# Instance normalisation: deeper lag between loads and stores, two-pass variance, and work taken off GpSimd

## The chip, the cores and the metric

The kernel runs on one core of one Trainium2 chip. The metric is the device time of one execution in microseconds (us). The profile's span is about 1.8 us shorter than that time, because it leaves out what lies around the program.

## The reference, cut to what matters

```python
x = randn(8, 64, 32, 64, 64), float32          # 512 instances of 131072 elements
mean = x.mean over the last three axes
var = x.var over the last three axes
out = (x - mean) / sqrt(var + 1e-5)            # float32
```

The input is 268.4 MB and so is the output. Every element has to come in once and go out once: 536.9 MB.

## The kernel before

Both kernels cut the data in the same way. An instance is spread over 16 partitions, 8192 elements on each, so that a tile of 128 partitions by 8192 elements holds 8 instances and 4 MB. There are 64 tiles. Each is loaded, normalised in place and stored. Loads and stores are all issued on one queue, SyncE's. (The profile has short names for the engines: SP is SyncE, DVE VectorE, ACT ScalarE, POOL GpSimd, PE TensorE and PEld its weight loads; a q behind a name is the part of an engine that waits and issues.)

```python
    LAG = 2
    # ... cut ...
    data_pool = ctx.enter_context(tc.tile_pool(name="data", bufs=4))
    # ... cut ...
    c1 = F // 8
    c2 = F // 4
    norm_splits = [
        (nc.vector, 0, c1),
        (nc.scalar, c1, c2),
        (nc.gpsimd, c2, F),
    ]

    def issue_load(g):
        x_tiles = data_pool.tile([P, KPG, F], fp32, name="x_tiles")
        src = x_packed[g * KPG : (g + 1) * KPG].rearrange("k p f -> p k f")
        nc.sync.dma_start(out=x_tiles, in_=src)
        return x_tiles
    # ... cut ...
        for k in range(KPG):
            nc.vector.reduce_sum(
                out=psums[:, k, 0:1],
                in_=x_tiles[:, k, :],
                axis=mybir.AxisListType.X,
            )
    # ... cut ...
            nc.scalar.activation(
                out=sq_scratch,
                in_=x_tiles[:, k, :],
                func=mybir.ActivationFunctionType.Square,
                accum_out=psums[:, k, 1:2],
            )

```

The sum of every partition comes from VectorE and the sum of squares from ScalarE. A matmul with a block pattern adds up the 16 partitions of an instance and spreads the result over them. Six small operations make `scale` and `bias` (cut here). Then three engines share the normalisation, GpSimd with three quarters of the columns:

```python
        for k in range(KPG):
            for eng, lo, hi in norm_splits:
                if eng is nc.scalar:
                    nc.scalar.activation(
    # ... cut ...
                    )
                else:
                    eng.tensor_scalar(
                        out=x_tiles[:, k, lo:hi],
    # ... cut ...
                    )

    def issue_store(g, x_tiles):
        dst = out_packed[g * KPG : (g + 1) * KPG].rearrange("k p f -> p k f")
        nc.sync.dma_start(out=dst, in_=x_tiles)

    pending = {}
    for g in range(n_groups):
        x_tiles = issue_load(g)
        issue_compute(g, x_tiles)
        pending[g] = x_tiles
        if g >= LAG:
            issue_store(g - LAG, pending.pop(g - LAG))
    for g in range(n_groups - LAG, n_groups):
        issue_store(g, pending.pop(g))
```

The store of tile g-2 stands in the queue behind the load of tile g, and four tiles fit in the buffers.

## Time and profile before

| | before |
|---|---|
| time, median of 3 runs | 1251.63 us (1251.09 to 1252.23) |
| span of the profiled run | 1249.7 us |
| VectorE, ScalarE, GpSimd busy | 53%, 44%, 30% |
| the queue's transfers, share of 16 DMA engines' span | 99.7% |
| one tile in the steady state | 19.37 us = 8.39 MB at 433 GB/s |

These lines are from the page of the kernel before. They give the span; each engine's busy time; the DMA queue with its packets, megabytes and share of 16 DMA engines' time; and the three costliest groups of instructions: busy time, mean of one in ns, idle time just before them and what ended it.

```profile
span 1249.7 us, 1827 instructions
...
PE 35.7 (3%) x128; PEld 32.1 (3%) x128; DVE 659.2 (53%) x449; ACT 550.6 (44%) x258; POOL 380.3 (30%) x70
...
q1 hardware_dynamic: 18432, 536.88, 99.7%
...
L92 DVE TENSOR_REDUCE psums<-x_tiles 128x1 f32<-128x8192 f32 x64 | 555.9, 8686 | 492.9 <-DMA x_tiles<-in_x_dram 492.9
L100 ACT ACTIVATE sq_scratch<-x_tiles 128x8192 bf16<-128x8192 f32 x64 | 449.9, 7029 | 461.3 <-DMA x_tiles<-in_x_dram 461.3
L169 POOL TENSOR_SCALAR x_tiles<-x_tiles,scale,bias 128x6144 f32<-128x6144 f32 x64 | 379.4, 5929 | 855.4 <-DVE bias L149 634.4
```

No compute engine is full and the DMA engines are. The two engines that open a tile wait for loads (492.9 and 461.3 us in all).

The waits of the queue's own issuing engine in the kernel before (instruction, what it waited for, us in all, times, longest):

```profile
SPq L85 <- DMA out_dram<-x_tiles: 700.8, 60, 12.6
SPq L180 <- POOL x_tiles L169: 303.9, 64, 4.8
```

Loads (L85) wait until an earlier store has left its buffer. Stores (L180) wait for the engines that normalise, mostly GpSimd.

The end of the kernel before, in order of time: the last tile's part on GpSimd, and the last three stores, the last of them issued at the end of the interval, 1198.00 + 39.04 = 1237.04 us. It has to wait for GpSimd.

```profile
1198.00 39.04 SPq L180 DMA_DIRECT2D out_dram<-x_tiles  x3
...
1230.76 5.93 POOL L169 TENSOR_SCALAR x_tiles<-x_tiles,scale,bias 128x6144 f32<-128x6144 f32 x1 [13.42 <-ACT std L141]
```

And this is the table of windows of the kernel before. Its last two columns: the busy share of the 16 DMA engines, as a mean over the engines, and GB/s. (A packet counts in the window where it starts, so short windows scatter, and can show more than 1.)

```profile
core 0: us, PE busy (x) PEld busy (x) DVE busy (x) ACT busy (x) POOL busy (x), PEclk, DMA share, GB/s
0.00:60.00 60.00, 1.67 (x6) 1.50 (x6) 37.50 (x23) 34.66 (x15) 18.92 (x9) 1.00 0.98 410
60.00:500.00 440.00, 12.83 (x46) 11.53 (x46) 230.31 (x161) 190.41 (x92) 135.40 (x23) 1.00 1.00 432
...
1233.00:1237.00 4.00, 0.00 (x0) 0.00 (x0) 0.00 (x0) 0.00 (x0) 3.69 (x1) 1.00 0.31 131
1237.00:1241.00 4.00, 0.00 (x0) 0.00 (x0) 0.00 (x0) 0.00 (x0) 0.00 (x0) 1.00 0.92 393
1241.00:1245.00 4.00, 0.00 (x0) 0.00 (x0) 0.00 (x0) 0.00 (x0) 0.00 (x0) 1.00 1.22 524
1245.00:1249.00 4.00, 0.00 (x0) 0.00 (x0) 0.00 (x0) 0.00 (x0) 0.00 (x0) 1.00 0.36 156
```

From 1233 to 1237 us, while GpSimd finishes the last tile, the mean share is 0.31.

### The profile page before, as it was taken

To read this page: it belongs to the slowest core of one execution; us is meant where nothing else is said; L and a number is where in the kernel's file an instruction comes from. 1 tells how busy PE (TensorE), PEld (TensorE's weight loads), DVE (VectorE), ACT (ScalarE), POOL (GpSimd) and SP (SyncE) were. 2 spreads that over 40 slices of the span, in tenths; PEclk is the share of its full clock that TensorE was granted. 3 is DMA by queue.
4 is the path that set the end of the run, shared out by engine and by line. 5 is a ranking of instruction groups with operands and counts; after the bars stand their busy time and mean duration, and the time that the engine had idled before them with its cause. 6 is when DMAs were issued, how large, how long until landed. Compare 5 with 4: busy or idle time off the path is not lost.

```text
span 1249.7 us, 1827 instructions
## 1 busy us (share of the span) xinstructions
PE 35.7 (3%) x128; PEld 32.1 (3%) x128; DVE 659.2 (53%) x449; ACT 550.6 (44%) x258; POOL 380.3 (30%) x70
## 2 busy tenths in 40 slices
PE   0000000000000000000000000000000000000000
PEld 0000000000000000000000000000000000000000
DVE  5736455464554645546546455464554645646543
ACT  5535445354453544535435344354453544534432
POOL 2332332313323233232331322313323233132231
DMA  9999999999999999999999999999999999999998
GB/s 403 417 434 434 427 433 430 432 435 430 429 432 434 432 435 429 434 433 434 434 431 433 431 434 434 435 430 432 434 433 436 429 433 434 433 434 435 429 433 357
DMA packets 18444, 536.99 MB, mean 430 GB/s; under 512 B 2048, under 2 KB 2048, under 8 KB 2048
## 3 DMA queue, kind: packets, MB, share of 16 engines
q1 hardware_dynamic: 18432, 536.88, 99.7%
q14 instruction: 11, 0.09, 0.0%
q8 instruction: 1, 0.02, 0.0%
HBM read 268.44 MB, written 268.44 MB: 430 GB/s over the span
## 4 chain that ended last, share of the span: by engine, by line
DMA 74%; issue 16%; POOL 7%; DVE 1%; POOLq 1%; PE 0%; ACT 0%
DMA out_dram<-x_tiles 39%; DMA x_tiles<-in_x_dram 35%; POOL x_tiles L169 7%; DVE psums L92 1%; POOLq L221 0%; DVE x_tiles L169 0%; POOLq L169 0%; PE tot L108 0%; ACT std L141 0%; DVE scale L147 0%; DVE msq L128 0%; DVE me L117 0%; DVE bias L149 0%; DVE var_eps L131 0%
## 5 line engine op out<-in xcount | busy, mean ns | idle before, releaser
L92 DVE TENSOR_REDUCE psums<-x_tiles 128x1 f32<-128x8192 f32 x64 | 555.9, 8686 | 492.9 <-DMA x_tiles<-in_x_dram 492.9
L100 ACT ACTIVATE sq_scratch<-x_tiles 128x8192 bf16<-128x8192 f32 x64 | 449.9, 7029 | 461.3 <-DMA x_tiles<-in_x_dram 461.3
L169 POOL TENSOR_SCALAR x_tiles<-x_tiles,scale,bias 128x6144 f32<-128x6144 f32 x64 | 379.4, 5929 | 855.4 <-DVE bias L149 634.4
L161 ACT ACTIVATE x_tiles<-x_tiles,bias,scale 128x1024 f32<-128x1024 f32 x64 | 79.4, 1241 | 40.5 <-DVE bias L149 40.5
L141 ACT ACTIVATE std<-var_eps 128x1 f32<-128x1 f32 x64 | 13.0, 203 | 178.7 <-DVE var_eps L131 178.7
L108 PE MATMUL tot<-psums,ones_t 128*128 128x2 f32 x128 | 35.7, 348 | 1193.5 <-DVE psums L92 1193.5
L108 PEld LDWEIGHTS tot<-psums,ones_t 128*128 128x128 f32 x128 | 32.1, 311 | 1197.1 <-issue 1197.1
L169 DVE TENSOR_SCALAR x_tiles<-x_tiles,scale,bias 128x1024 f32<-128x1024 f32 x64 | 52.1, 813 | 2.5
L117 DVE TENSOR_SCALAR me<-tot 128x2 f32<-128x2 f32 x64 | 10.2, 160 | 47.5 <-PE tot L108 47.5
L147 DVE RECIPROCAL scale<-std 128x1 f32<-128x1 f32 x64 | 10.5, 164 | 21.8 <-ACT std L141 21.8
L100 ACT ACTIVATION_READ_ACCUMULATOR sq_scratch<-x_tiles 128x1 f32 x64 | 11.9, 187 | 0.0
L128 DVE TENSOR_TENSOR msq<-me 128x1 f32<-128x1 f32 x64 | 10.2, 159 | 2.2
L131 DVE SCALAR_TENSOR_TENSOR var_eps<-me,msq 128x1 f32<-128x1 f32 x64 | 10.2, 159 | 2.2
L149 DVE SCALAR_TENSOR_TENSOR bias<-me,scale 128x1 f32<-128x1 f32 x64 | 10.2, 159 | 2.2
L100 ACT ACT_TABLE_LOAD x1 | 1.3, 1283 | 0.8 <-PEq L207 0.8
L141 ACT ACT_TABLE_LOAD x1 | 1.3, 1283 | 0.0
L51 DVE MEMSET ones_t<- 128x128 f32 x1 | 0.2, 165 | 0.9 <-PEq L207 0.9
L53 POOL TENSOR_SCALAR_AFFINE_SELECT ones_t<-ones_t 128x128 f32<-128x128 f32 x1 | 0.3, 343 | 0.6 <-DVE ones_t L51 0.6
L62 POOL TENSOR_SCALAR_AFFINE_SELECT ones_t<-ones_t 128x128 f32<-128x128 f32 x1 | 0.3, 338 | 0.1
L207 POOL MEMSET const-float32-0.0<- 128x1 f32 x1 | 0.1, 98 | 0.3 <-issue 0.3
L207 POOL MEMSET const-bfloat16-1.0<- 128x1 bf16 x1 | 0.1, 101 | 0.0
L207 POOL MEMSET const-uint8-127<- 128x1 uint8 x1 | 0.1, 101 | 0.0
(1 smaller groups left out, 0.1 us busy)
## 6 DMA issues: line engine op xcount, KB each, us to landing
x_tiles<-in_x_dram SPq DMA_DIRECT2D x64, 4096.0 KB, 29.0
out_dram<-x_tiles SPq DMA_DIRECT2D x64, 4096.0 KB, 31.5
```

The source lines that it names most:

```text
L92: nc.vector.reduce_sum(out=psums[:, k, 0:1], in_=x_tiles[:, k, :], axis=mybir.AxisListType.X,)
L100: nc.scalar.activation(out=sq_scratch, in_=x_tiles[:, k, :], func=mybir.ActivationFunctionType.Square, accum_out=psums[:, k, 1:2],)
L108: nc.tensor.matmul(out=tot, lhsT=ones_t, rhs=psums, start=True, stop=True,)
L117: nc.vector.tensor_scalar(out=me2, in0=tot, scalar1=inv_F, scalar2=None, op0=mybir.AluOpType.mult,)
L128: nc.vector.tensor_mul(out=msq, in0=mean, in1=mean)
L131: nc.vector.scalar_tensor_tensor(out=var_eps, in0=e2, scalar=eps_f, in1=msq, op0=mybir.AluOpType.add, op1=mybir.AluOpType.subtract,)
L141: nc.scalar.activation(out=std, in_=var_eps, func=mybir.ActivationFunctionType.Sqrt,)
L147: nc.vector.reciprocal(out=scale, in_=std)
L149: nc.vector.scalar_tensor_tensor(out=bias, in0=mean, scalar=-1.0, in1=scale, op0=mybir.AluOpType.mult, op1=mybir.AluOpType.mult,)
L161: nc.scalar.activation(out=x_tiles[:, k, lo:hi], in_=x_tiles[:, k, lo:hi], func=mybir.ActivationFunctionType.Identity, scale=scale[:, k : ...
L169: eng.tensor_scalar(out=x_tiles[:, k, lo:hi], in0=x_tiles[:, k, lo:hi], scalar1=scale[:, k : k + 1], scalar2=bias[:, k : k + 1], op0=mybir ...
L207: nc = _bacc.Bacc("TRN2", target_bir_lowering=False, num_devices=1)
```

## The change

The intent is a shorter chain from a loaded tile to a ready one, GpSimd out of the stream, a variance computed from differences (meant to be more exact than E[x²] - mean²; not compared here), and more room between a load and its store: six buffers, and the store of tile g-4 behind the load of tile g. The instructions stand on every engine in program order.

```diff
-    LAG = 2                      (four data buffers)
+    SLOTS = 6                    (six data buffers)
...
-    nc.vector.reduce_sum(psums[:, k, 0:1], x_tiles)            # all columns
-    nc.scalar.activation(sq_scratch, x_tiles, Square, accum_out=psums[:, k, 1:2])
-    matmul, then me2, msq, var_eps, std (Sqrt), scale, bias
+        nc.vector.reduce_sum(out=sums[:, 0:1], in_=t[:, :cut])         # cut = F // 2
+        nc.scalar.activation(out=unused[:, cut:], in_=t[:, cut:],
+                             func=Act.Identity, accum_out=sums[:, 1:2])
+        nc.tensor.matmul(out=mean_ps, lhsT=avg, rhs=sums, start=True, stop=True)
+        nc.vector.tensor_reduce(out=neg_mean, in_=mean_ps, op=Alu.add, negate=True)
+        nc.scalar.activation(out=unused, in_=t, func=Act.Square,
+                             bias=neg_mean, accum_out=squares)
+        nc.tensor.matmul(out=var_ps, lhsT=avg, rhs=squares, start=True, stop=True)
+        nc.scalar.activation(out=std, in_=var_ps, func=Act.Sqrt, bias=eps_t)
+        nc.vector.reciprocal(out=scale, in_=std)
+        nc.vector.tensor_mul(out=bias, in0=neg_mean, in1=scale)
-    normalise: VectorE 1/8, ScalarE 1/8, GpSimd 3/4 of the columns
+        nc.vector.tensor_scalar(t[:, cut:], scale, bias)               # half
+        nc.scalar.activation(t[:, :cut], Identity, scale, bias)        # half
...
+    LAG = 4
+    with tc.manual_schedule():
+        for g in range(n_tiles + LAG):
+            if g < n_tiles:
+                tiles[g] = load(g)
+                compute(tiles[g])
+            if g >= LAG:
+                nc.sync.dma_start(out=out_t[g - LAG], in_=tiles.pop(g - LAG))
```

(Arguments are shortened, and cuts are marked with "..." .)

More of the change, by code (lines that the diff above doesn't have):

```diff
@@ L4 @@
 import concourse.tile as tile
-from concourse import bass_utils, mybir
+from concourse import mybir
 from concourse._compat import with_exitstack
@@ L18 @@
     fp32 = mybir.dt.float32
+    Alu = mybir.AluOpType
+    Act = mybir.ActivationFunctionType
     P = 128
@@ L29 @@
     F = n_elem // SPLIT
-    G = 8
-    KPG = G // IPT
-    n_groups = n_inst // G
-    LAG = 2
-    x_packed = x.rearrange("b c d h w -> (b c) (d h w)").rearrange(
+    n_tiles = n_inst // IPT
+    SLOTS = 6
+    x_t = x.rearrange("b c d h w -> (b c) (d h w)").rearrange(
         "(k i) (s f) -> k (i s) f", i=IPT, s=SPLIT
     )
-    out_packed = out.rearrange("b c d h w -> (b c) (d h w)").rearrange(
+    out_t = out.rearrange("b c d h w -> (b c) (d h w)").rearrange(
         "(k i) (s f) -> k (i s) f", i=IPT, s=SPLIT
@@ L44 @@
     singles = ctx.enter_context(tc.tile_pool(name="singles", bufs=1))
-    data_pool = ctx.enter_context(tc.tile_pool(name="data", bufs=4))
-    scratch_pool = ctx.enter_context(tc.tile_pool(name="scratch", bufs=2))
+    data_pool = ctx.enter_context(tc.tile_pool(name="data", bufs=SLOTS))
     stat_pool = ctx.enter_context(tc.tile_pool(name="stats", bufs=4))
-    psum_pool = ctx.enter_context(tc.tile_pool(name="psum", bufs=4, space=bass.MemoryType.PSUM))
-    ones_t = singles.tile([P, P], fp32)
-    nc.vector.memset(ones_t, 1.0 / SPLIT)
-    blk_pattern = [[-SPLIT, P // SPLIT], [0, SPLIT]]
+    psum_pool = ctx.enter_context(
+        tc.tile_pool(name="psum", bufs=2, space=bass.MemoryType.PSUM)
+    )
+    avg = singles.tile([P, P], fp32, name="avg")
+    nc.vector.memset(avg, 1.0 / n_elem)
     nc.gpsimd.affine_select(
-        out=ones_t,
-        in_=ones_t,
-        pattern=blk_pattern,
-        compare_op=mybir.AluOpType.is_ge,
+        out=avg,
+        in_=avg,
+        pattern=[[-SPLIT, IPT], [0, SPLIT]],
+        compare_op=Alu.is_ge,
         fill=0.0,
@@ L62 @@
     nc.gpsimd.affine_select(
-        out=ones_t,
-        in_=ones_t,
-        pattern=[[SPLIT, P // SPLIT], [0, SPLIT]],
-        compare_op=mybir.AluOpType.is_ge,
+        out=avg,
+        in_=avg,
+        pattern=[[SPLIT, IPT], [0, SPLIT]],
+        compare_op=Alu.is_ge,
         fill=0.0,
@@ L70 @@
     )
-    inv_F = 1.0 / F
-    c1 = F // 8
-    c2 = F // 4
-    norm_splits = [
-        (nc.vector, 0, c1),
-        (nc.scalar, c1, c2),
-        (nc.gpsimd, c2, F),
-    ]
-    def issue_load(g):
-        x_tiles = data_pool.tile([P, KPG, F], fp32, name="x_tiles")
-        src = x_packed[g * KPG : (g + 1) * KPG].rearrange("k p f -> p k f")
-        nc.sync.dma_start(out=x_tiles, in_=src)
-        return x_tiles
-    def issue_compute(g, x_tiles):
-        psums = stat_pool.tile([P, KPG, 2], fp32, name="psums")
-        for k in range(KPG):
-            nc.vector.reduce_sum(
-                out=psums[:, k, 0:1],
-                in_=x_tiles[:, k, :],
-                axis=mybir.AxisListType.X,
-            )
-            sq_scratch = scratch_pool.tile(
-                [P, F], mybir.dt.bfloat16, name="sq_scratch"
-            )
-            nc.scalar.activation(
-                out=sq_scratch,
-                in_=x_tiles[:, k, :],
-                func=mybir.ActivationFunctionType.Square,
-                accum_out=psums[:, k, 1:2],
-            )
-        tot = psum_pool.tile([P, KPG, 2], fp32, name="tot")
-        nc.tensor.matmul(
-            out=tot,
-            lhsT=ones_t,
-            rhs=psums,
-            start=True,
-            stop=True,
-        )
-        me2 = stat_pool.tile([P, KPG, 2], fp32, name="me2")
-        nc.vector.tensor_scalar(
-            out=me2,
-            in0=tot,
-            scalar1=inv_F,
-            scalar2=None,
-            op0=mybir.AluOpType.mult,
-        )
-        mean = me2[:, :, 0]
-        e2 = me2[:, :, 1]
-        msq = stat_pool.tile([P, KPG], fp32, name="msq")
-        nc.vector.tensor_mul(out=msq, in0=mean, in1=mean)
-        var_eps = stat_pool.tile([P, KPG], fp32, name="var_eps")
-        nc.vector.scalar_tensor_tensor(
-            out=var_eps,
-            in0=e2,
-            scalar=eps_f,
-            in1=msq,
-            op0=mybir.AluOpType.add,
-            op1=mybir.AluOpType.subtract,
-        )
-        std = stat_pool.tile([P, KPG], fp32, name="std")
-        nc.scalar.activation(
-            out=std,
-            in_=var_eps,
-            func=mybir.ActivationFunctionType.Sqrt,
-        )
-        scale = stat_pool.tile([P, KPG], fp32, name="scale")
-        nc.vector.reciprocal(out=scale, in_=std)
-        bias = stat_pool.tile([P, KPG], fp32, name="bias")
-        nc.vector.scalar_tensor_tensor(
-            out=bias,
-            in0=mean,
-            scalar=-1.0,
-            in1=scale,
-            op0=mybir.AluOpType.mult,
-            op1=mybir.AluOpType.mult,
-        )
-        for k in range(KPG):
-            for eng, lo, hi in norm_splits:
-                if eng is nc.scalar:
-                    nc.scalar.activation(
-                        out=x_tiles[:, k, lo:hi],
-                        in_=x_tiles[:, k, lo:hi],
-                        func=mybir.ActivationFunctionType.Identity,
-                        scale=scale[:, k : k + 1],
-                        bias=bias[:, k : k + 1],
-                    )
-                else:
-                    eng.tensor_scalar(
-                        out=x_tiles[:, k, lo:hi],
-                        in0=x_tiles[:, k, lo:hi],
-                        scalar1=scale[:, k : k + 1],
-                        scalar2=bias[:, k : k + 1],
-                        op0=mybir.AluOpType.mult,
-                        op1=mybir.AluOpType.add,
-                    )
@@ L178, in issue_store @@
-    def issue_store(g, x_tiles):
-        dst = out_packed[g * KPG : (g + 1) * KPG].rearrange("k p f -> p k f")
-        nc.sync.dma_start(out=dst, in_=x_tiles)
-    pending = {}
-    for g in range(n_groups):
-        x_tiles = issue_load(g)
-        issue_compute(g, x_tiles)
-        pending[g] = x_tiles
-        if g >= LAG:
-            issue_store(g - LAG, pending.pop(g - LAG))
-    for g in range(n_groups - LAG, n_groups):
-        issue_store(g, pending.pop(g))
+    eps_t = singles.tile([P, 1], fp32, name="eps_t")
@@ new lines, with load, compute @@
+    nc.vector.memset(eps_t, eps_f)
+    unused = singles.tile([P, F], mybir.dt.uint8, name="unused")
+    def load(g):
+        t = data_pool.tile([P, F], fp32, name="xt")
+        nc.sync.dma_start(out=t, in_=x_t[g])
+        return t
+    def compute(t):
+        cut = F // 2
+        sums = stat_pool.tile([P, 2], fp32, name="sums")
+        nc.vector.reduce_sum(
+            out=sums[:, 0:1], in_=t[:, :cut], axis=mybir.AxisListType.X
+        )
+        nc.scalar.activation(
+            out=unused[:, cut:],
+            in_=t[:, cut:],
+            func=Act.Identity,
+            accum_out=sums[:, 1:2],
+        )
+        mean_ps = psum_pool.tile([P, 2], fp32, name="mean_ps")
+        nc.tensor.matmul(out=mean_ps, lhsT=avg, rhs=sums, start=True, stop=True)
+        neg_mean = stat_pool.tile([P, 1], fp32, name="neg_mean")
+        nc.vector.tensor_reduce(
+            out=neg_mean,
+            in_=mean_ps,
+            axis=mybir.AxisListType.X,
+            op=Alu.add,
+            negate=True,
+        )
+        squares = stat_pool.tile([P, 1], fp32, name="squares")
+        nc.scalar.activation(
+            out=unused, in_=t, func=Act.Square, bias=neg_mean, accum_out=squares
+        )
+        var_ps = psum_pool.tile([P, 1], fp32, name="var_ps")
+        nc.tensor.matmul(out=var_ps, lhsT=avg, rhs=squares, start=True, stop=True)
+        std = stat_pool.tile([P, 1], fp32, name="std")
+        nc.scalar.activation(out=std, in_=var_ps, func=Act.Sqrt, bias=eps_t)
+        scale = stat_pool.tile([P, 1], fp32, name="scale")
+        nc.vector.reciprocal(out=scale, in_=std)
+        bias = stat_pool.tile([P, 1], fp32, name="bias")
+        nc.vector.tensor_mul(out=bias, in0=neg_mean, in1=scale)
+        nc.vector.tensor_scalar(
+            out=t[:, cut:],
+            in0=t[:, cut:],
+            scalar1=scale,
+            scalar2=bias,
+            op0=Alu.mult,
+            op1=Alu.add,
+        )
+        nc.scalar.activation(
+            out=t[:, :cut], in_=t[:, :cut], func=Act.Identity, scale=scale, bias=bias
+        )
@@ L194 @@
+    LAG = 4
+    tiles = {}
+    with tc.manual_schedule():
[5 more added lines that the diff above has]
+                nc.sync.dma_start(out=out_t[g - LAG], in_=tiles.pop(g - LAG))
 _INS = ['x', 'eps']
```

## The prediction

> **What bounds the kernel now.** The 16 DMA engines. The page's slice table shows DMA at nine tenths in all slices but the last; the queue table gives the one SP queue 99.7% of 16 engines' span, 536.9 MB at a mean 430 GB/s. No compute engine is near full (VectorE 53%, ScalarE 44%, GpSimd 30%); VectorE's big reductions idle 493 us waiting for loads (groups table). In the timeline a tile takes 19.37 us (reductions at 600.16 and 1219.84, 32 tiles apart): 8.39 MB per tile, 433 GB/s. The Trainium skill, "DMA: Bandwidth & Descriptors", section "Where 436 GB/s comes from", gives a fabric ceiling of 435.2 GB/s; this trace agrees. At that ceiling the bytes alone take 1233.6 us, so no schedule of the same bytes gains 2%.
>
> **Where the rest goes (windows table).** Start: 2 us before full rate; from 2 to 60 us a mean near 417 GB/s, some 2 us lost, part of it where three loads are done and the first store is only just issued (30 us). End: from 1233 to 1237 the DMA share is 0.31, because the last store waits for tile 63's chain (reduction 8.69, matmul and small operations 1.9, GpSimd 5.93 us): about 3 us lost. After the last packets near 1247.3 come 2.4 us of completion.
>
> **What the change does.** Bytes, packets, queue: unchanged. GpSimd's normalisation and the single-pass square go; sums and normalisation are split in halves over VectorE and ScalarE; the square needs the mean. Tiles follow one another in program order; only the next tile's sums start as each engine gets free. Estimates from before's durations:
> - sums: VectorE 4096 of 8192 elements, 4.4 us; ScalarE 3.8 us (1241 ns for 1024 and 7029 ns for 8192: about 0.83 ns each)
> - matmul, negated mean: 0.95 us
> - ScalarE square with accumulator read: 7.3 us
> - matmul, square root, reciprocal, bias: 1.45 us
> - normalisation: ScalarE half 3.8 us (VectorE half 2.3 to 3.2)
>
> The loop closes through ScalarE: 3.8 + 0.95 + 7.3 + 1.45 + 3.8 = 17.3 us per tile, 15.2 of them ScalarE (78% of the span). That is 2 us under the DMA's 19.37, so the chain stays hidden. The order on each engine shows two activation-table loads in all, so none in the chain.
>
> **On the critical path.** Only start and end. Five loads run unbroken (49 us) while tile 0 is ready near 31 us, so the dip goes. In steady state both kernels keep two or more 4 MB transfers queued: same rate. At the end stores 59 to 62 (39 us of DMA) stand between the last load and the last store and cover tile 63's 17 us: the hole goes. Gain 3.5 to 5 us, 0.3 to 0.4%.
>
> **Predicted: 1247.5 us, 8 in 10 between 1241 and 1252.** Faster by over 2%: 0.01; within 2%: 0.96; slower: 0.03.
>
> **What would show it.** DMA share about 99.8%; no hole before the last store; 19.3 to 19.4 us per tile; ScalarE 75 to 80% busy, VectorE near 40%, GpSimd near zero; ScalarE's sums waiting 1.5 to 2.5 us per tile for the load once the initial backlog is worked off; SP waiting on stores landing, hardly on compute.
>
> **What would make it wrong.** A compute chain over 19.4 us (slower VectorE half, long semaphore hops) would make it compute-bound with DMA share below 95%: 20 us per tile would be about 1290. Another DMA rate, from the all-load start, the all-store end or the other spacing of loads and stores, would move it by some 0.3% either way.

## The result

| | before | after |
|---|---|---|
| median of the runs made together (4 each) | 1251.66 us | 1251.43 us (1251.12 to 1251.57) |
| ratio after/before | | 0.9997, 95% interval 0.9983 to 1.0011 |
| span of the profiled run | 1249.7 us | 1249.9 us |
| VectorE, ScalarE, GpSimd busy | 53%, 44%, 30% | 37%, 77%, 0% |
| last store issued | 1237.04 us | 1218.83 us |

A ratio here was made, with its interval, from the fast runs of both kernels in the same rounds, so it is not quite the ratio of the medians. The time lies inside the predicted range (1241 to 1252), and "the same within 2%" was right. But the gain of 3.5 to 5 us that the prediction counted on is not there: it is 0.2 us, with an interval from 2.1 us faster to 1.4 us slower. That the time still lies in the range is no support for this gain: the range reached up to the time of the kernel before.

The same lines of the page, for the kernel after:

```profile
span 1249.9 us, 1770 instructions
...
PE 73.7 (6%) x256; PEld 64.1 (5%) x256; DVE 467.1 (37%) x322; ACT 960.3 (77%) x386; POOL 0.9 (0%) x6
...
q1 hardware_dynamic: 18432, 536.88, 99.7%
...
L103 ACT ACTIVATE unused<-xt,neg_mean 128x8192 uint8<-128x8192 f32 x64 | 455.8, 7122 | 99.5 <-DVE neg_mean L95 99.5
L83 DVE TENSOR_REDUCE sums<-xt 128x1 f32<-128x4096 f32 x64 | 282.8, 4419 | 156.3 <-DMA xt<-in_x_dram 156.3
L86 ACT ACTIVATE unused<-xt 128x4096 uint8<-128x4096 f32 x64 | 231.3, 3614 | 84.8 <-DMA xt<-in_x_dram 84.8
```

The compute side came out as foreseen. ScalarE is the busiest engine and still waits for loads (84.8 us at its first instruction of a tile). The first instruction of the second and third tile on ScalarE in the kernel after (start, duration), and then of two tiles of the steady state (in brackets the idle time before and what ended it):

```profile
31.40 3.60 ACT L86 ACTIVATE unused<-xt 128x4096 uint8<-128x4096 f32 x1
...
48.37 3.60 ACT L86 ACTIVATE unused<-xt 128x4096 uint8<-128x4096 f32 x1
```

```profile
600.43 3.62 ACT L86 ACTIVATE unused<-xt 128x4096 uint8<-128x4096 f32 x1 [1.56 <-DMA xt<-in_x_dram]
...
619.75 3.62 ACT L86 ACTIVATE unused<-xt 128x4096 uint8<-128x4096 f32 x1 [1.48 <-DMA xt<-in_x_dram]
```

From 31.40 to 48.37 us is 16.97 us, the chain of one tile without waiting for a load. In the steady state a tile comes every 19.3 to 19.4 us, and ScalarE idles 1.5 us for it.

The queue's own waits and its last issues in the kernel after. Long waits of stores for compute are left at six stores (83.2 us in all; before, 303.9 us at all 64 for GpSimd alone), and the last five stores are all issued by 1172.09 + 46.74 = 1218.83 us, 18 us earlier than before:

```profile
SPq L77 <- DMA out_dram<-xt: 1069.7, 58, 19.5
SPq L135 <- DVE xt L114: 83.2, 6, 26.9
```

```profile
1172.09 46.74 SPq L135 DMA_DIRECT2D out_dram<-xt  x5
```

And the same table of windows, for the kernel after:

```profile
0.00:60.00 60.00, 2.91 (x10) 2.51 (x10) 19.20 (x14) 43.03 (x17) 0.89 (x6) 1.00 0.97 411
60.00:500.00 440.00, 28.41 (x98) 24.55 (x98) 176.53 (x123) 360.54 (x148) 0.00 (x0) 1.00 1.00 432
...
1233.00:1237.00 4.00, 0.00 (x0) 0.00 (x0) 0.00 (x0) 0.00 (x0) 0.00 (x0) 1.00 1.02 442
1237.00:1241.00 4.00, 0.00 (x0) 0.00 (x0) 0.00 (x0) 0.00 (x0) 0.00 (x0) 1.00 0.95 410
1241.00:1245.00 4.00, 0.00 (x0) 0.00 (x0) 0.00 (x0) 0.00 (x0) 0.00 (x0) 1.00 0.59 254
1245.00:1249.00 4.00, 0.00 (x0) 0.00 (x0) 0.00 (x0) 0.00 (x0) 0.00 (x0) 1.00 0.19 82
```

The hole between 1233 and 1237 us is gone (1.02 instead of 0.31), exactly as predicted. In its place the share falls off at the end: 0.59 and 0.19 between 1241 and 1249 us, with nothing left to issue and nothing to wait for. The start is no better either: 411 GB/s over the first 60 us against 410. So the question is where the 3 us of the hole went.

### What a mean over 16 engines hides

A transfer of this kernel is carried by all 16 DMA engines, eight packets of 32 KB on each. The Trainium skill, "DMA: Bandwidth & Descriptors", section "Why a DMA increments its semaphore by 16 and not by 1", says that every engine that takes part adds its own increment to the transfer's semaphore (the counter that a waiting engine watches) when its share has landed. The trace agrees: it holds 2048 such landings for 128 transfers, 16 for each. They do not say which engine each came from, but the first and the last of the 16 can be read for every transfer. This table is worked out from those records (in us of the span; the zero of each run is set by the first transfer's last landing, which released the first instruction, or, where nothing is computed, by the 0.84 us that lie between the last landing and the end of the span):

```
                        transfer before the last      last transfer
                        first engine, last engine     first engine, last engine
before                  1233.35       1239.17         1247.65       1248.83
after                   1233.09       1239.37         1242.77       1249.03
```

In the kernel before the fastest engine was done with the store of tile 62 at 1233.35 us and then waited for the last store, issued at 1237.04. The slowest engine was done with tile 62 only at 1239.17 us, 2.1 us after the last store had been issued. It ended the last store at 1248.83, 9.66 us later, which is the steady time of one transfer (9.68 us). It never waited: there is no room for a wait in 9.66 us. (That the same engine was last both times is inferred from this, as the records name none.) The hole was made of the faster engines' spare time.

In the kernel after no engine waits. The fastest ends at 1242.77 us and the slowest at 1249.03. The spare time of the faster engines has moved from before the last store to behind it.

The same records show when the slowest falls behind. The lag of the slowest engine behind the fastest (from here on "lag"; the `LAG` of the kernels, in tiles, is another thing), in us, at the n-th transfer of 128:

```
n                0     8    16    32    48    64    96   126
before         0.68  2.33  3.47  5.41  5.72  5.73  5.72  5.82
after          0.42  0.93  3.20  5.47  6.30  6.27  6.29  6.27
```

The engines drift apart in the first 450 us or so, up to about 6 us, and then stay as they are. Both kernels do it in the same way.

The packet records show how. The median packet of 32 KB takes 1213 ns in both kernels. Packets that take over 20 ns more: in the first 60 us 60 of them with 28.4 us in all before, and 36 with 22.2 us after; from 60 to 500 us 70 with 18.4 us before, and 96 with 20.8 us after; from 500 to 1210 us 6 with 2.2 us before and 12 with 2.4 us after. In the kernel before they come mostly once per 19.4 us, in the kernel after less regularly. The records name no engine, but packets can be joined end to start into 16 nearly gapless chains; counted along those chains, 83 of the 92 slow packets of before that come after 60 us, and 83 of 108 of after, are the last two of a load or the first two of the store behind it. The place in the chain is thus inferred; the durations are measured.

**Theory A:** the time is that of the DMA engine that falls furthest behind. What happens to the other fifteen, the hole included, costs nothing. **Rival B:** the hole was lost transfer time, as I had predicted, and the change loses as much elsewhere. For the drift itself: **theory D1**, it is made where a load is followed by a store; **rival D2**, it comes with time, whatever is carried.

### The profile page after: what moved, and what is told of

It is laid out like the page before. It is cut to its first block, busy times and chain, and to the rows that moved or that the text cites. A ratio compares the mean times of both kernels' runs of the same rounds, so it can differ in the third digit from the quotient of the medians.

```text
span 1249.9 us, 1770 instructions
## 1 busy us (share of the span) xinstructions
PE 73.7 (6%) x256; PEld 64.1 (5%) x256; DVE 467.1 (37%) x322; ACT 960.3 (77%) x386; POOL 0.9 (0%) x6
## 2 busy tenths in 40 slices
DMA packets 18443, 536.99 MB, mean 430 GB/s; under 512 B 2048, under 2 KB 2048, under 8 KB 2048
## 4 chain that ended last, share of the span: by engine, by line
DMA 89%; ACT 5%; DVE 1%; SPq 1%; issue 0%; PE 0%; ACTq 0%
DMA out_dram<-xt 86%; DMA xt<-in_x_dram 3%; ACT unused L103 3%; ACT xt L122 2%; ACT unused L86 1%; SPq L77 1%; DVE sums L83 1%; PE mean_ps L93 0%; PE var_ps L107 0%; ACT std L109 0%; ACT L109 0%; DVE scale L111 0%; DVE bias L113 0%; DVE neg_mean L95 0%; SPq L135 0%
## 5 line engine op out<-in xcount | busy, mean ns | idle before, releaser
L103 ACT ACTIVATE unused<-xt,neg_mean 128x8192 uint8<-128x8192 f32 x64 | 455.8, 7122 | 99.5 <-DVE neg_mean L95 99.5
L83 DVE TENSOR_REDUCE sums<-xt 128x1 f32<-128x4096 f32 x64 | 282.8, 4419 | 156.3 <-DMA xt<-in_x_dram 156.3
L86 ACT ACTIVATE unused<-xt 128x4096 uint8<-128x4096 f32 x64 | 231.3, 3614 | 84.8 <-DMA xt<-in_x_dram 84.8
L122 ACT ACTIVATE xt<-xt,bias,scale 128x4096 f32<-128x4096 f32 x64 | 243.3, 3802 | 30.4 <-DVE bias L113 30.4
L114 DVE TENSOR_SCALAR xt<-xt,scale,bias 128x4096 f32<-128x4096 f32 x64 | 154.4, 2413 | 2.7 <-DVE bias L113 0.3
L93 PE MATMUL mean_ps<-sums,avg 128*128 128x2 f32 x128 | 36.1, 352 | 655.3 <-DVE sums L83 539.4
L107 PE MATMUL var_ps<-squares,avg 128*128 128x1 f32 x128 | 37.6, 362 | 484.9 <-ACT unused L103 484.9
L93 PEld LDWEIGHTS mean_ps<-sums,avg 128*128 128x128 f32 x128 | 32.0, 311 | 659.2 <-ACT unused L86 641.7
L107 PEld LDWEIGHTS var_ps<-squares,avg 128*128 128x128 f32 x128 | 32.1, 311 | 490.4 <-ACT unused L103 490.4
L109 ACT ACTIVATE std<-var_ps,eps_t 128x1 f32<-128x1 f32 x64 | 16.7, 261 | 42.6 <-PE var_ps L107 42.6
```

The source lines that it names most:

```text
L83: nc.vector.reduce_sum(out=sums[:, 0:1], in_=t[:, :cut], axis=mybir.AxisListType.X)
L86: nc.scalar.activation(out=unused[:, cut:], in_=t[:, cut:], func=Act.Identity, accum_out=sums[:, 1:2],)
L93: nc.tensor.matmul(out=mean_ps, lhsT=avg, rhs=sums, start=True, stop=True)
L103: nc.scalar.activation(out=unused, in_=t, func=Act.Square, bias=neg_mean, accum_out=squares)
L107: nc.tensor.matmul(out=var_ps, lhsT=avg, rhs=squares, start=True, stop=True)
L109: nc.scalar.activation(out=std, in_=var_ps, func=Act.Sqrt, bias=eps_t)
```

## The experiments

Twelve kernels were run. Times are medians; ratios are against the kernel before in the same rounds. The edits of the first three are to the kernel before, the rest to the kernel after.

### 1. Fill the hole in the kernel before

```diff
+    last_splits = [(nc.vector, 0, F // 2), (nc.scalar, F // 2, 3 * F // 4),
+                   (nc.gpsimd, 3 * F // 4, F)]
-            for eng, lo, hi in norm_splits:
+            for eng, lo, hi in (last_splits if g == n_groups - 1 else norm_splits):
```

> The kernel before, with only the last tile's normalisation re-split (VectorE half, ScalarE and GpSimd a quarter each), so that the last store is issued about 3.4 us earlier and the hole in the mean DMA share (1233 to 1237) is filled. Theory A (the slowest of the 16 DMA engines sets the time; the hole is only the faster engines waiting, the slowest was still on the store before): no change, within 0.5 us. Rival B (the hole is lost DMA time, as the prediction had it, and the change lost as much elsewhere): about 3 us faster than before, 1248.6.

Measured: 1251.83 us, ratio 0.9998 (0.9984 to 1.0012). The last store came only 1.6 us earlier (1235.46), not 3.4, for a reason that the last lines of this run's timeline show:

```profile
1230.77 2.41 DVE L175 TENSOR_SCALAR x_tiles<-x_tiles,scale,bias 128x4096 f32<-128x4096 f32 x1
...
1230.98 4.12 POOL L175 TENSOR_SCALAR x_tiles<-x_tiles,scale,bias 128x2048 f32<-128x2048 f32 x1 [13.48 <-ACT std L147]
1235.13 0.33 SPq L186 DMA_DIRECT2D out_dram<-x_tiles  x1
```

GpSimd took 4.12 us for a quarter of the columns, where 5.93 us had been enough for three quarters. The Trainium skill, "SBUF — State Buffer", section "SBUF: two separate sides", says that VectorE in a two-port mode and GpSimd lock each other out of a shared port for whole instructions. This trace agrees: VectorE ended at 1233.18 us, and GpSimd went on for 1.92 us, about what 2048 columns take it alone (in run 3 below a pass over 6144 columns, with VectorE idle, took 5.31 us; a third of it is 1.77). The windows of this run at its end:

```profile
1233.00:1237.00 4.00, 0.00 (x0) 0.00 (x0) 0.18 (x1) 0.01 (x1) 2.11 (x1) 1.00 0.76 328
...
1245.00:1249.00 4.00, 0.00 (x0) 0.00 (x0) 0.00 (x0) 0.00 (x0) 0.00 (x0) 1.00 0.17 74
```

The hole is mostly filled (0.76 instead of 0.31), and the end shows what was gained: 0.17 instead of 0.36 in the last window, and no earlier finish. The slowest engine landed tile 62 at 1239.39 us and tile 63 at 1249.07, 9.68 us later. The interval of the time is too wide to exclude a gain of 1.6 us; the landings of the profiled run exclude it there, as its slowest engine had no wait to lose.

### 2. Issue the last store 1 us later

```diff
+    last_splits = [(nc.vector, 0, c1), (nc.gpsimd, c1, F)]      # last tile only
```

> The kernel before, with the last tile's ScalarE part of the normalisation given to GpSimd: last store issued about 1.0 us later. Theory A: within 0.5 us of before, as the slowest engine has about 1.6 us of earlier store left when the last store is issued. Rival B: 1.0 us slower.

Measured: 1251.48 us, ratio 0.9998 (0.9985 to 1.0010). GpSimd's part took 6.79 us instead of 5.93, so the store was 0.9 us later than it would have been. The slowest engine landed tile 62 at 1238.57 and tile 63 at 1248.21, 9.64 us later: still no wait. It is as A has it, but 0.9 us is within the interval, so the time alone does not decide.

### 3. Issue it 6 us later

```diff
+        if g == n_groups - 1:
+            nc.gpsimd.tensor_scalar(out=x_tiles[:, 0, c2:F], in0=x_tiles[:, 0, c2:F],
+                                    scalar1=1.0, scalar2=0.0, op0=mult, op1=add)
```

> The kernel before, with one more GpSimd pass (times 1.0) over the last tile: last store issued about 5.9 us later. Theory A: about 4.3 us slower (5.9 less the slack of about 1.6). Rival B: 5.9 us slower.

Measured: 1256.12 us, ratio 1.0035 (1.0023 to 1.0048), which is 4.4 us. The extra pass took 5.31 us, and the last store was issued at 1242.87, 5.83 us later than before. The windows of its end:

```profile
1233.00:1237.00 4.00, 0.00 (x0) 0.00 (x0) 0.00 (x0) 0.00 (x0) 4.00 (x1) 1.00 0.34 147
1237.00:1241.00 4.00, 0.00 (x0) 0.00 (x0) 0.00 (x0) 0.00 (x0) 3.91 (x2) 1.00 0.02 8
1241.00:1245.00 4.00, 0.00 (x0) 0.00 (x0) 0.00 (x0) 0.00 (x0) 1.51 (x1) 1.00 0.62 262
```

Now there is a real hole, with a share of 0.02. The slowest engine was done with tile 62 at 1239.58 us and so did wait; all 16 engines landed the last store within 0.14 us of each other, at 1253.62. That is 4.8 us after before's end, 1.0 us less than the delay, because the first part of the delay was only the faster engines' time. A expected 4.3, B 5.9. The interval of the time (2.9 to 6.0 us) holds both; the landings fit A with a smaller slack than it had named. Here, where every engine waited, the store landed 10.75 us after its issue (1242.87 to 1253.62); in the kernel before, the slowest engine landed it 11.79 us after (1237.04 to 1248.83). So the last store could have come about 1.0 us later there at no cost, where A had said 1.6. The 0.9 us of run 2 lie just within it.

### 4. The kernel after with the old lag and buffers

```diff
-    SLOTS = 6
+    SLOTS = 4
-    LAG = 4
+    LAG = 2
```

> The kernel after, with the store lag back at two tiles and four buffers. Its chain from load to ready tile is 17.9 us against 16.9 us before, so the last store comes about 1 us later than in the kernel before. Theory A: within 1 us of before and after. Rival B: the hole is back and the kernel is 3 to 4 us slower than after (which was 1251.4).

Measured: 1253.18 us, ratio 1.0011 (0.9999 to 1.0024). It is a miss for both: the median is 1.7 us above before's and after's, where A had said within 1 us and B 3 to 4 us. The landings say that the last store was not the reason: the slowest engine landed tile 62 at 1240.59 and tile 63 at 1250.25, 9.66 us later (and 1.2 us behind that of the kernel after). It was behind from the start: 95 slow packets with 38.5 us in the first 60 us, against 36 with 22.2 us in the kernel after. But the kernel before has the same lag and buffers, with 60 slow packets and 28.4 us there, so what made this start slower is not shown. It is one profile, and the ratio's interval still touches no difference.

### 5. No computing at all

```diff
-                compute(tiles[g])
```

> The kernel after with all computing taken out (copies x, wrong on purpose), same loads, stores, buffers and order. Theory A (the DMA stream alone, as its slowest engine runs it, sets the time): the same as after, within 1 us, with the same ragged end of 5 to 6 us. Rival (computing costs something through waits or through contention for the on-chip memory): 3 us or more faster.

Measured: 1251.48 us, ratio 0.9995 (0.9980 to 1.0011). Loads, stores, order and buffers alone take the whole time. The windows of this run (no compute columns, as nothing runs there):

```profile
core 0: us, DVE busy (x) POOL busy (x), PEclk, DMA share, GB/s
0.00:60.00 60.00, 0.17 (x2) 0.89 (x6) 1.00 0.97 411
...
1241.00:1245.00 4.00, 0.00 (x0) 0.00 (x0) 1.00 0.49 213
1245.00:1249.00 4.00, 0.00 (x0) 0.00 (x0) 1.00 0.08 33
```

The end is as ragged as in the kernel after, with 5.6 us between the first engine's last landing and the last engine's; the first 60 us are the same 411 GB/s. So the computing of the kernel after, about 17 us for each tile, costs nothing, neither through waits nor by slowing a transfer. The Trainium skill, "SBUF — State Buffer", section "SBUF: two separate sides", says that a DMA cannot be slowed by a compute operation; this run agrees within 0.2%. (The comparison with the reference called the output correct, though the kernel only copies: instances of 131072 normal numbers have a mean near 0 and a variance near 1. It would not notice a lost normalisation here.)

Theory A stands: this run shows that the stream of loads and stores alone sets the time, and the landings in runs 1 to 3 show that within it the slowest engine does.

### 6 and 7. Loads alone, and stores alone

```diff
-    (the loop)
+        for g in range(n_tiles):            # run 6, then six stores
+            tiles[g] = load(g)
...
+        for g in range(n_tiles):            # run 7, after six loads
+            nc.vector.memset(tiles[g % SLOTS][:, 0:1], 0.0)
+            nc.sync.dma_start(out=out_t[g], in_=tiles[g % SLOTS])
```

The memset is there so that a store waits for the one six before it. Their outputs are wrong, which doesn't matter for the times.

> 64 loads without computing, then 6 stores (wrong on purpose). Theory D1 (the engines drift apart because packets at the change from a load to a store run slow): with one such change in all, the 16 engines stay within 1 us of each other, packets keep 1213 ns, and the DMA share drops from 1.0 to 0 within about 1 us at the end; about 70 x 9.68 + 4 = 682 us. Rival D2 (engines drift with time, whatever they carry): a ragged end of 3 to 6 us, as in both kernels.

> 6 loads, then 64 stores of the same six tiles (wrong on purpose). D1: sharp end within about 1 to 2 us, about 682 us. D2: ragged end of 3 to 6 us.

Measured: 686.01 and 686.07 us (spans 684.3 and 684.4). The lag of the slowest engine never passed 0.94 us with loads and 0.92 us with stores. Between 60 us and the end the loads had no slow packet before their change to stores; the stores had 177, but with 27 ns on average, 4.8 us over all engines. The end of the run with the loads:

```profile
678.00:680.00 2.00, 0.00 (x0) 0.00 (x0) 1.00 1.02 442
680.00:682.00 2.00, 0.00 (x0) 0.00 (x0) 1.00 0.83 360
682.00:684.00 2.00, 0.00 (x0) 0.00 (x0) 1.00 0.00 0
```

The share goes from full to none within 2 us, instead of falling over 6. D2 falls: transfers in one direction did not drive the engines apart in over 600 us. So D1 holds as far as it goes.

It does not go all the way. The one turn from loads to stores in run 7, at 60 us, cost 19 slow packets with 11.3 us, like the first turn in both kernels. The one turn in run 6, at about 622 us, cost nothing: no packet there took over 1228 ns, although the engines were within 1 us of each other and turned together. Not every turn is slow, and I have no run that says which are.

### 8. The change of direction half as often

```diff
-            store of tile g-4 behind the load of tile g
+        for g in range(0, n_tiles, 2):      # two stores, then two loads
+            for h in (g, g + 1):
+                nc.sync.dma_start(out=out_t[h], in_=tiles.pop(h))
+            for h in (g + LAG, g + LAG + 1):
+                if h < n_tiles: tiles[h] = load(h); compute(tiles[h])
```

> The kernel after with loads and stores in pairs (two stores, two loads): half as many changes of direction. D1: the drift builds up at half the rate (about 3 us behind at 450 us instead of 6), and the end is 0 to 3 us earlier than after. D2: no difference.

Measured: 1255.03 us, ratio 1.0026 (1.0014 to 1.0039): slower, where D1 had promised 0 to 3 us less. The drift was slower, as expected (lag at transfers 16, 32, 64, 96 and 126: 1.00, 2.65, 5.66, 8.32 and 9.27 us, against 3.20, 5.47, 6.27, 6.29 and 6.27 in the kernel after). But it did not stop at 6 us. I had taken 6 us for a fixed limit. It is not: with runs of 19.4 us in one direction the lag reaches 9.3 us, and it was still growing a little at the end. The slowest engine's last transfer again began without a wait (1242.73 to 1252.40).

### 9. Twice as often, in halves

```diff
+            for lo in (0, H):               # H = F // 2: column halves, alternating
+                load half of tile g; store half of tile g - LAG
```

> The kernel after with every load and store cut in two column halves, alternating: packets of 16 KB, a change of direction every 4.84 us instead of 9.68. If the drift grows until the engines are spread over some share of one transfer (about 6 of 9.68 us in both kernels), it ends near 3 us and the kernel is about 3 us faster than after, 1248.5. If the drift is a fixed 6 us, or a packet has a fixed cost of its own (16 KB packets over 606 ns), it is the same or slower (6 ns more a packet would be 6 us).

Measured: 1256.50 us, ratio 1.0038 (1.0024 to 1.0052). The lag stood at 3.4 us in the first half of the run and at 4.7 us in the second, against 6.3, so shorter runs do keep the engines closer. But packets of 16 KB take 611 ns (the median), more than half of 1213, and in the steady state a transfer of half a tile takes 4.862 us, where half of 9.68 is 4.84: over 256 of them 5.6 us. The packets' own cost is more than the closer engines bring.

### 10. Two queues: stores from GpSimd

```diff
-                nc.sync.dma_start(out=out_t[g - LAG], in_=tiles.pop(g - LAG))
+                nc.gpsimd.dma_start(out=out_t[g - LAG], in_=tiles.pop(g - LAG))
```

The Trainium skill, "DMA: Bandwidth & Descriptors", section "Queues, rings and completion order", says that a DMA engine serves the queues it has work for in turn, packet by packet. If so, loads and stores alternate after every packet and there are no long runs in one direction any more. The trace of this run agrees for its packets of 32 KB: where one can be joined end to start to the next without ambiguity, from 60 to 1200 us, the next is of the other queue in 1988 of 2280 cases.

> The kernel after with the stores issued by the idle GpSimd (a second queue), so that loads and stores share every DMA engine packet by packet instead of in runs of eight packets. Theory D1 in its milder form (a packet is slow only while many engines turn from load to store together): steady period stays near 19.36 us per tile. If every turn costs, the period is longer. The stores no longer wait behind loads, so the last tile's 17 us chain and store come with little else left to move: 5 to 15 us slower than after in all.

Measured: 1252.27 us, ratio 0.9999 (0.9982 to 1.0015). The feared 5 to 15 us did not come: load and store share the engines evenly, so a store takes 47 us to land, about two stores are always left behind the last load, and the last tile's chain is covered. From 60 to 500 us there were 22 slow packets with 1.4 us (96 with 20.8 us in the kernel after); the lag was 1.1 us at transfer 32, but it grew slowly to the end, to 4.3 us at 126. The data was there 1.9 us earlier than in the kernel after (last landing at 1247.12), but 3.4 us passed from there to the end of the span, against 0.84 us with one queue of SyncE. In this trace GpSimd's own closing instruction (DRAIN) ended only at 1249.78 us, 2.7 us after that landing, and the other engines' closing instructions came after it.

### 11. Half of the engines a little ahead from the start

```diff
-        nc.sync.dma_start(out=t, in_=x_t[g])
+        cuts = (0, 8, 16, P) if g == 0 else (0, P)      # tile 0 in 8, 8 and 112 partitions
+        for lo, hi in zip(cuts[:-1], cuts[1:]):
+            nc.sync.dma_start(out=t[lo:hi], in_=x_t[g][lo:hi])
```

> The kernel after with tile 0's load cut so that half of the engines carry nine packets of it and half seven: the two halves then turn about 2.4 us apart from the start. Milder D1: fewer slow packets in the first 450 us and less of a further drift; the time stays within 1.5 us of after, since the engines with nine packets have 1.2 us more to do. If the slow packets come from something else, their sum does not change.

Measured: 1265.31 us, ratio 1.0104 (1.0089 to 1.0120): a failure. The first 30 us ran at 118, 233 and 295 GB/s for 10 us each, with a DMA share of 0.84 to 0.96 and packets of up to 4.4 us (2.2 us at most in the kernel after). The odd split of the first tile costs more than anything it could show, so the run does not tell anything about the drift. Why those packets are so slow is open.

### 12. Two queues: stores from ScalarE

```diff
-                (store of tile g - 4 on SyncE's queue)
+            nc.scalar.dma_start(out=out_t[g], in_=t)        # behind its own half of tile g
```

> The kernel after with each store issued by ScalarE right after its own half of the normalisation: two queues as in the run with GpSimd's, without GpSimd in the stream. In that run slow packets vanished after the first 60 us, 15 of 16 engines ended within 1.3 us of each other and the last packet ended at 1246.1, but 4.5 us more passed to the end of the span and the period was 19.43 us per tile. If those 4.5 us belong to GpSimd's queue and the mixed directions keep the engines together here too: about 1247.5 us, 3 to 4 us faster than before and after, with 15 or 16 engines ending within 1.5 us. If the drift comes back or the period lengthens: 1250 or more.

Measured: 1249.30 us (1249.17 to 1249.47), ratio 0.9977 (0.9963 to 0.9990). It beats the kernel before by 2.8 us in the medians of the same rounds, and 0.23% in the ratio: small, and clear of the noise. I had expected 3 to 4 us: right in sign, somewhat less in size. The kernel after was not in these rounds; it equals before within 0.2%, and the fastest of its four runs (1251.12) is slower than the slowest of these five (1249.47). (The tail of 4.5 us in my expectation was misread: the last packet of run 10 ended at 1246.63 us, not 1246.1, and landed at 1247.12.) One store and the tiles around it, on ScalarE:

```profile
611.88 0.34 ACTq L131 DMA_DIRECT2D out_dram<-xt  x1
613.48 3.62 ACT L86 ACTIVATE unused<-xt 128x4096 uint8<-128x4096 f32 x1 [1.63 <-DMA xt<-in_x_dram]
...
632.82 3.62 ACT L86 ACTIVATE unused<-xt 128x4096 uint8<-128x4096 f32 x1 [1.49 <-DMA xt<-in_x_dram]
```

The issue costs ScalarE 0.34 us per tile, out of time in which it would have waited for the load anyway. The end of the run:

```profile
1237.00:1241.00 4.00, 0.00 (x0) 0.00 (x0) 0.00 (x0) 0.00 (x0) 0.00 (x0) 1.00 0.93 401
1241.00:1245.00 4.00, 0.00 (x0) 0.00 (x0) 0.00 (x0) 0.00 (x0) 0.00 (x0) 1.00 0.67 287
1245.00:1249.00 4.00, 0.00 (x0) 0.00 (x0) 0.00 (x0) 0.00 (x0) 0.00 (x0) 1.00 0.02 8
```

The share is gone 2 us earlier than in the kernel after (0.02 instead of 0.19 from 1245 us on). From 60 to 500 us there were 4 slow packets with 1.0 us. The lag was 0.7 us at transfer 16, 1.2 at 32 and 3.9 at 126; the last landing was at 1246.94 us, 2.1 us before that of the kernel after. The 0.84 us from there to the end are as with SyncE's queue alone, so the 3.4 us of run 10 go with GpSimd's queue. The mean of the 16 engines' last landings moved by only 0.3 us (1244.99 in the kernel after, 1244.66 here), so of the 2.1 us that the last one gained, 1.8 come from the engines ending closer together. This run also drops `LAG`: a store no longer stands behind four later loads. Run 10 kept that order and gained 1.9 us at the last landing, so most of it goes with the second queue; the two were not separated further. And the lag grew to the end here too; the 28 slow packets between 500 and 1210 us add 3.2 us over all engines, and the records do not tell whether they lie on one.

## Why the prediction was right or wrong, point by point

- *DMA-bound, 433 GB/s, no gain of 2% possible.* Right. Without any computing the time is 1251.48 us, and steady state ran at 433 GB/s. (The prediction's 1233.6 us is an estimate from the ceiling that it cites; no run shows that time.)
- *The compute chain takes 17.3 us per tile, ScalarE 15.2 of them, and stays hidden under 19.37.* Right: 16.97 us, ScalarE busy 960.3 us over 64 tiles = 15.0 us, 77% of the span, with 1.5 us of idle time per tile.
- *"the hole goes"* Right as a fact: 0.31 became 1.02.
- *"from 1233 to 1237 the DMA share is 0.31, because the last store waits for tile 63's chain ... about 3 us lost", and from it "Gain 3.5 to 5 us".* This is the step that failed. The share is a mean over 16 engines. The slowest of them was still on the store of tile 62 until 1239.17 us, 2.1 us after the last store's issue. The runs that filled the hole or deepened it by 0.9 us left the time as it was. What was lost there was the spare time of faster engines; the term is 0 and not 3 us. The "2.4 us of completion" after 1247.3 us are a like misreading: 1247.29 is where the last packet began; it ended at 1248.50, and from its landing to the end of the span it is 0.84 us.
- *"Start: ... some 2 us lost, part of it where three loads are done and the first store is only just issued ... so the dip goes."* Wrong in the same sum. The first 60 us run at 411 GB/s after the change and at 410 before it, and at 411 with no computing. With loads alone they run at 419. The change of direction costs there: slow packets add 28.4 us before and 22.2 us after, over 16 engines, and with loads alone 9.6 us, all of them in the first 20 us. The late first store was not the cause of most of it.
- *"Another DMA rate, from the all-load start, the all-store end or the other spacing ... would move it by some 0.3% either way."* It named the right place, but as a rate of the whole. What is there is a drift between engines, about equal in both kernels (5.8 and 6.3 us).

Settled: the slowest DMA engine sets the time, and the engines stayed within 1 us of each other with transfers in one direction, while they drifted by 4.7 to 9.3 us where loads and stores alternated in runs on one queue. Not settled: with loads and stores mixed packet by packet on two queues they drifted more slowly, but to 4.3 and 3.9 us, so long runs are not the whole cause. Open: what makes a packet slow, and why the turn of run 6 cost nothing; what drives the slow drift of runs 10 and 12; whether it is always the same engine that ends last (the records name none); and why the lag that is reached grows with the length of a run in one direction (3.4 to 4.7, 6.3 and 9.3 us for runs of 4.84, 9.68 and 19.4 us).

## What to carry to other kernels

When a DMA-bound kernel shows a hole in the mean DMA share, look at the first and the last engine's landing of the transfers around it before counting the hole as time: if the slowest engine runs through it, filling it gains nothing. Take out the computing once; if the time stays, no work on the compute side, however good, can show. And when loads and stores alternate on one queue, try giving the stores to the queue of an engine that has spare time: here, on ScalarE, it was worth 0.2% against the kernel before, where the whole change showed no gain. On GpSimd's queue the time stayed as it was (0.9999), as the end took longer.

## What the Trainium skill lacked or had wrong

- "DMA: Bandwidth & Descriptors", sections "Issuing engines are not separate DMA queues" and "Rules for kernel authors": issuing DMAs from several engines is said to bring no bandwidth, only the time of the issue. Nearly so, but not quite here: with stores from ScalarE's queue instead of SyncE's the time was 0.9977 (0.9963 to 0.9990) of before. The 16 engines stay closer together there (lag 1.2 us instead of 5.5 at transfer 32, 3.9 instead of 6.3 at 126); that this is the cause is argued from the landings of run 12.
- The same page has nothing on DMA engines drifting apart when loads and stores alternate on one queue: about 6 us over the first 450 us with 4 MB transfers, 9.3 us with pairs of them, 3.9 to 4.3 us with two queues, under 1 us with transfers in one direction. I found it on no other page either.
- The same page, section "Where 436 GB/s comes from", gives 435.2 GB/s as the ceiling. That is neither lacking nor wrong: the steady 433 GB/s here agrees (32 KB in 1210 ns on each of 16 engines). Over the whole program, start and end included, the mean is 430.
- No page that I read gives the cost of ending on GpSimd's queue: 3.4 us from the last landing to the end of the span, against 0.84 us with SyncE's or ScalarE's.
- No page that I read explains why a first load split into 8, 8 and 112 partitions leaves the first 30 us of the run at 118 to 295 GB/s.
